# Forgetting attention with both heads' halves in one stationary block: the value product of the second head group reshaped

## The chip, the cores and the metric

The kernel runs on one core of one Trainium2 chip. The metric is the device time of one execution in microseconds. TensorE (PE) multiplies a stationary block, loaded into its array beforehand, by moving columns and writes into PSUM banks. VectorE (DVE) and ScalarE (ACT) work on PSUM and SBUF, GpSimd (POOL) on SBUF, and SyncE (SP) issues nearly all transfers.

## The reference, cut to what matters

One decoder layer on 256 tokens of width 2048: a combined input projection, two groups of 16 attention heads of 64 channels, an output projection, a gated feed-forward part with a short convolution, and norms around each. The second group, called fox in the code, is forgetting attention:

```python
def forgetting_attention(q, k, v, log_f):
    c = lax.cumsum(log_f, axis=1)
    ...
        s = jnp.einsum('bqhd,bshd->bhqs', q_blk, k).astype(jnp.float32) * scale
        s = s + c_blk[..., None] - cT[:, :, None, :]
        s = jnp.where((q_pos[:, None] >= k_pos[None, :])[None, None], s, -jnp.inf)
        p = jax.nn.softmax(s, axis=-1)
        return jnp.einsum('bhqs,bshd->bqhd', p.astype(v.dtype), v)
...
    o_b = rmsnorm(o_b.reshape(B, S, D_FOX), grp_fox_g[l])
    mix = jnp.concatenate([o_a, o_b], axis=-1) @ w_out[l]
```

## The kernel before

Every float32 operand of a matmul is split into a high part (`hi`, a rounded copy) and a low part (`lo`, what is left), and a product is summed from the passes high by high, high by low and low by high. The weights go this way too: SP loads a unit of 128x1024 into `raw` (`w_load`, L69; five buffers), ACT casts it into `whi` (L112, five buffers), DVE subtracts and writes `wlo` (L115), PE uses both.

TensorE's order is the order in which the code is written (it is scheduled by hand); the other engines' queues are ordered by the framework's scheduler, and each engine works through its own queue strictly in order. Attention is woven into the projections: `tick()` is called every few matmuls, and `later(n, f)` runs `f` after n more ticks. For a pair of heads `attend` registers four steps: `tables` (POOL builds the additive table in `p`), `scores` (L475, then softmax on DVE and ACT), `transposes` (probabilities turned by PE, L510, and split into high `ph`, L312, and low `pl`, L313), and `pv` (values times probabilities). For the fox group, two pairs at a time follow a q and a k projection of 256 columns each (`proj_T`); after the fourth two, the remaining steps run inside `out_half(0)`, the first half of the output projection. There a weight unit is 12 matmuls of 512 columns, with a tick after the sixth and the last. Steps of one pair use rotating PSUM banks of the tag `att`, four in all.

In `pv` of a fox pair, `weighted` before the change uses as stationary block the values of both heads (2 x 64 channels), high or low, and as moving columns both heads' probabilities (2 x 256 queries; in the second key block 2 x 128). Three passes over two key blocks are six matmuls (L534, L536) into one bank. Of its four quarters the two in which head and probability belong together are used. ACT then writes the gained high part into `oT` (L545) and the square into `sqo` (L546), DVE the low part of `oT` (L547), each once per head on 64 partitions, and POOL adds the square to `sqs` (L553). The first attention group already has `shared` value heads: four matmuls (L522, L524), ACT copies the lower half of the bank into `olow` (L527), DVE adds halves (L530), and then the same chain on 128 partitions.

When all fox pairs are done, `group_rstd(1)` sums `sqs` over channels with four small matmuls (L681). It is registered four ticks after the last `pv`:

```python
        later(stages(6, 1)[2] + 4, lambda: group_rstd(1, rstd_b))
```

After `out_half(0)` the attention pool is given back. `gbc_mix` (L726) is laid into its room, and `x_sb` (L729, two loads) into that of the values `vpb`; both are loaded by SP, in the same queue as the weight units.

Of the kernel before, what the change touches and what calls it, by code (L numbers as in the profile page):

```python
# [8 lines left out]
F32 = mybir.dt.float32  # L9
F32R = mybir.dt.float32r  # L10
BF16 = mybir.dt.bfloat16
AF = mybir.ActivationFunctionType
ALU = mybir.AluOpType
# [4 lines left out]
P = 128  # L18
# [13 lines left out]
def hybrid_layer(ctx: ExitStack, tc: tile.TileContext, x, pre_mix_g, w_in, b_forget, sinks,  # L32
# [3 lines left out]
    pe, act, dve, pool, sp = nc.tensor, nc.scalar, nc.vector, nc.gpsimd, nc.sync  # L36
# [12 lines left out]
    def bank(tag="acc"):  # L49
        return ps.tile([P, 512], F32, tag=tag, bufs=4, name="bank_" + tag)  # L50
# [264 lines left out]
    with tc.tile_pool(name="mixp", bufs=1) as mp:  # L315
# [110 lines left out]


        vpa = ap.tile([P, 2, 2, P], F32R, tag="vpa", name="vpa")
        vpb = main.tile([P, 2, 2, 8, P], F32R, tag="x", name="vpb")

        NK = 3
        keys = ap.tile([P, 2 * NK, S], F32R, tag="keys", name="keys")
# [26 lines left out]
        def attend(j, q, ki, values, table, h0, sink, at, shared=False):  # L459


            qh, ql = q
            kh, kl = khi[ki], klo[ki]
            st = {}

            def scores():


                p = st["p"]
                sb = [bank("att") for _ in range(2)]  # L470
                passes = ((qh, kh), (ql, kh), (qh, kl))
                for cs, t, nk in ((slice(0, 256), 1, 256), (slice(256, 384), 0, P)):
                    for n, (a, b) in enumerate(passes):
                        for e, r in enumerate(halves):
                            pe.matmul(sb[e][:, cs], a[r, t * P:(t + 1) * P], b[r, 0:nk],  # L475
                                      start=(n == 0), stop=(n == 2))

                nm = small.tile([P, 2, 2], F32, tag="nm", name="nm")
                for t, cs in tiles:
                    for e in range(2):  # L480
                        dve.tensor_tensor_reduce(
                            p[:, e, cs], sb[e][:, cs], p[:, e, cs], -1.0,
                            nsnk[:, h0 + e:h0 + e + 1] if sink else -NEG,
                            ALU.add, ALU.min, nm[:, t, e:e + 1])
                rs = small.tile([P, 2, 2], F32, tag="rs", name="rs")
                if sink:
                    es = small.tile([P, 2, 2], F32, tag="es", name="es")
                    sk = snk[:, h0:h0 + 2].unsqueeze(1).to_broadcast([P, 2, 2])
                    dve.tensor_tensor(es, nm, sk, op=ALU.add)
                    act.activation(es, es, AF.Exp)  # L490
                for t, cs in tiles:
                    for e in range(2):
                        act.activation(p[:, e, cs], p[:, e, cs], AF.Exp, bias=nm[:, t, e:e + 1],
                                       scale=-1.0, accum_out=rs[:, t, e:e + 1])
                if sink:
                    dve.tensor_tensor(rs, rs, es, op=ALU.add)
                dve.reciprocal(rs, rs)
                for t, cs in tiles:
                    for e in range(2):
                        dve.tensor_scalar(p[:, e, cs], p[:, e, cs], rs[:, t, e:e + 1], None,  # L500
                                          op0=ALU.mult)

            def transposes():
                p = st["p"]
                st["h"] = ap.tile([P, 2, 384], F32R, tag="ph", name="ph")
                st["l"] = ap.tile([P, 2, 384], F32R, tag="pl", name="pl")
                for e in range(2):
                    pb = bank("att")
                    for i, c in enumerate((256, 0, P)):
                        pe.transpose(pb[:, i * P:(i + 1) * P], p[:, e, c:c + P], ident)  # L510
                    split(st["h"][:, e, :], st["l"][:, e, :], pb[:, :384])

            def weighted():

                ph, pl = st["h"], st["l"]
                o = bank("att")
                ov = o.rearrange("p (e q) -> p e q", e=2)
                first, second = slice(0, 256), slice(256, 384)
                if shared:

                    for n, p in enumerate((ph, pl)):
                        pe.matmul(ov, values(0), p[:, :, first], start=(n == 0), stop=False)  # L522
                    for n, p in enumerate((ph, pl)):
                        pe.matmul(ov[:, :, P:256], values(1), p[:, :, second], start=False,  # L524
                                  stop=(n == 1))
                    low = ap.tile([64, 2, 256], F32, tag="olow", name="olow")
                    act.copy(low, ov[64:128])  # L527
                    s = scratch()
                    for e, r in enumerate(halves):
                        dve.tensor_tensor(s[r, :], ov[0:64, e, :], low[:, e, :], op=ALU.add)  # L530
                    return [(slice(0, P), s)]
                passes = ((0, ph), (1, ph), (0, pl))
                for n, (hl, p) in enumerate(passes):
                    pe.matmul(ov, values(hl, 0), p[:, :, first], start=(n == 0), stop=False)  # L534
                for n, (hl, p) in enumerate(passes):
                    pe.matmul(ov[:, :, P:256], values(hl, 1), p[:, :, second], start=False,  # L536
                              stop=(n == 2))
                return [(r, ov[r, e, :]) for e, r in enumerate(halves)]

            def pv():  # L540
                sq = ap.tile([P, 256], F32, tag="sqo", bufs=1, name="sqo")
                for r, o in weighted():
                    g = gcol[r, 32 + j:33 + j]
                    hi, lo = oT[j][r, 0:256], oT[j][r, 256:512]
                    act.activation(hi, o, AF.Copy, scale=g)  # L545
                    act.activation(sq[r, :], o, AF.Square)  # L546
                    dve.scalar_tensor_tensor(lo, o, g, hi.bitcast(F32), op0=ALU.mult,  # L547
                                             op1=ALU.subtract)
                acc = sqs[:, j // 8, :]
                if j % 8 == 0:  # L550
                    pool.tensor_copy(acc, sq)
                else:
                    pool.tensor_tensor(acc, acc, sq, op=ALU.add)  # L553

            def tables():
                st["p"] = ap.tile([P, 2, 384], F32, tag="p", bufs=2, name="p")
                table(st["p"])

            for n, f in zip((max(at[0] - 3, 1),) + at, (tables, scores, transposes, pv)):
                later(n, f)  # L560
# [14 lines left out]
        def fox_pair(p, q, ki, at):  # L575
            def table(t):
                cb = ap.tile([P, 2, 256], F32, tag="cb", bufs=2, name="cb")
                sp.dma_start(cb.rearrange("p e k -> p (e k)"),
                             c_dram[2 * p:2 * p + 2, :].rearrange("e k -> (e k)")
                             .partition_broadcast(P))  # L580
                for e in range(2):
                    h = 2 * p + e
                    pool.tensor_scalar(t[:, e, 0:256], cb[:, e, :], -1.0, cq[:, 1, h:h + 1],
                                       op0=ALU.mult, op1=ALU.add)
                    pool.tensor_scalar(t[:, e, 256:384], cb[:, e, 0:P], -1.0, cq[:, 0, h:h + 1],
                                       op0=ALU.mult, op1=ALU.add)

                v = t[:, :, P:384]
                pool.affine_select(out=v, in_=v, compare_op=ALU.is_ge, fill=NEG, base=0,
                                   pattern=[[0, 4], [-1, P]], channel_multiplier=1)  # L590

            attend(8 + p, q, ki, lambda hl, t: vpb[:, hl, t, p, :], table, 2 * p, False, at)

        def stages(n, m):
            return n, n + 6 + 3 * m, n + 9 + 4 * m
# [35 lines left out]
        for p0, npair, cols in ((0, 3, 384), (3, 3, 384), (6, 2, 272)):  # L631
# [11 lines left out]
                    if kt % 4 != 0:  # L643
                        tick()
            for t, b in enumerate(b2):
                bv = b[:, :npair * P].rearrange("p (j c) -> p j c", c=P)
                vh, vl = vpb[:, 0, t, p0:p0 + npair, :], vpb[:, 1, t, p0:p0 + npair, :]
                act.activation(vh, bv, AF.Copy, scale=rpre[t])
                dve.scalar_tensor_tensor(vl, bv, rpre[t], vh.bitcast(F32), op0=ALU.mult,
                                         op1=ALU.subtract)  # L650
                if cols == 272:
                    dve.scalar_tensor_tensor(z[:, t, :], b[:, 256:272], rpre[t], bfb,
                                             op0=ALU.mult, op1=ALU.add)
# [593 lines left out]
```

## Time and profile before

| | |
|---|---|
| median of 3 runs | 1063.57 us (1063.05 to 1065.51) |
| profiled execution, span from first to last instruction | 1062.6 us |
| busy: PE, PE weight loads, DVE, ACT, POOL | 1049.6, 914.6, 839.7, 639.1, 229.3 us |
| fox attention and what it is woven into | about 172 to 272 us of the span |
| mean granted TensorE clock | 0.996 |

The span is the profiled execution's own time; the median of the runs is 0.97 us more, which is what lies around it. In rows of the timeline the columns are start in us, length in us, engine, line, operation, output and inputs, shape and count; what stands in brackets is the idle time ahead and what ended it. Rows of matmuls overlap at their ends, so that the distance between two starts is the cost of one, not its length. In groups by line the last columns are busy time, mean length in ns, and idle time ahead.

### The profile page before, as it was taken

To read this page: it belongs to the slowest core of one execution; us is meant where nothing else is said; L and a number is where in the kernel's file an instruction comes from. 1 tells how busy PE (TensorE), PEld (TensorE's weight loads), DVE (VectorE), ACT (ScalarE), POOL (GpSimd) and SP (SyncE) were. 2 spreads that over 40 slices of the span, in tenths; PEclk is the share of its full clock that TensorE was granted. 3 is DMA by queue.
4 is the path that set the end of the run, shared out by engine and by line. 5 is a ranking of instruction groups with operands and counts; after the bars stand their busy time and mean duration, and the time that the engine had idled before them with its cause. 6 is when DMAs were issued, how large, how long until landed. Compare 5 with 4: busy or idle time off the path is not lost.

```text
span 1062.6 us, 16272 instructions
## 1 busy us (share of the span) xinstructions
PE 1049.6 (99%) x5890; PEld 914.6 (86%) x5890; DVE 839.7 (79%) x1369; ACT 639.1 (60%) x1096; POOL 229.3 (22%) x256
## 2 busy tenths in 40 slices
PE   9999999999999999999999999999999999999996
PEld 7889988888889888888888888888888888888885
DVE  5988887887467887787767999668778687789987
ACT  6767667776556765566655556446556565556551
POOL 4253335441022121211212000002121121200004
PEclk9999999999999999999999999999999999999998
DMA  8745566555773876656665666666566665656563
GB/s 280 217 120 168 162 209 202 165 170 162 282 236 107 280 231 187 193 180 185 211 188 188 193 204 206 213 196 190 169 209 188 197 197 180 194 179 200 194 242 121
DMA packets 154285, 207.08 MB, mean 195 GB/s; under 512 B 6845, under 2 KB 131037, under 8 KB 153181
## 3 DMA queue, kind: packets, MB, share of 16 engines
q1 hardware_dynamic: 153200, 203.37, 60.7%
q10 hardware_dynamic: 1004, 2.68, 0.6%
q8 instruction: 46, 0.75, 0.3%
q14 instruction: 35, 0.28, 0.1%
HBM read 201.68 MB, written 4.21 MB: 194 GB/s over the span
## 4 chain that ended last, share of the span: by engine, by line
PE 84%; DVE 9%; issue 2%; DMA 2%; ACT 2%; POOL 1%; DVEq 0%; SPq 0%; POOLq 0%; ACTq 0%
PE bank_acc L284 15%; PE bank_att L284 14%; PE bank_acc L309 12%; PE bank_att L967 9%; PE bank_acc L290 8%; PE bank_att L290 7%; PE bank_acc L253 7%; DVE wlo L313 4%; PE bank_acc L258 4%; PE bank_acc L967 2%; PE bank_att L475 1%; PE bank_att L510 1%; DVE wlo L115 1%; PE bank_acc L932 1%; DMA raw<-in_w_down_dram 1%
## 5 line engine op out<-in xcount | busy, mean ns | idle before, releaser
L115 DVE TENSOR_TENSOR wlo<-raw,whi 128x1024 fp32r<-128x1024 f32 (+3 forms) x271 | 328.5, 1224 | 127.0 <-ACT whi L112 118.4
L112 ACT CAST whi<-raw 128x1024 fp32r<-128x1024 f32 (+3 forms) x270 | 273.2, 1029 | 131.8 <-issue 88.8
L899 POOL TENSOR_TENSOR room<-room,rowf 128x256 f32<-128x256 f32 x88 | 100.3, 1160 | 393.9 <-DVE room L898 392.0
L284 PE MATMUL bank_acc<-hT,whi 128*128 128x512 f32 x736 | 173.3, 390 | 0.0
L284 PEld LDWEIGHTS bank_acc<-hT,whi 128*128 128x128 f32 x736 | 136.4, 188 | 27.4
L967 PE MATMUL bank_att<-whi,G 128*128 128x512 f32 x488 | 156.0, 389 | 0.0
L284 PE MATMUL bank_att<-hT,whi 128*128 128x512 f32 x640 | 150.6, 390 | 0.0
L284 PEld LDWEIGHTS bank_att<-hT,whi 128*128 128x128 f32 x640 | 118.7, 188 | 23.9
L967 PEld LDWEIGHTS bank_att<-whi,G 128*128 128x128 f32 x488 | 91.6, 188 | 18.9
L967 PE MATMUL bank_att<-wlo,G 128*128 128x512 f32 x244 | 95.0, 389 | 0.2 <-DVE wlo L313 0.2
L290 PEld LDWEIGHTS bank_acc<-hT,wlo 128*128 128x128 f32 x736 | 89.3, 188 | 2.0
L290 PE MATMUL bank_acc<-hT,wlo 128*128 128x256 f32 x736 | 89.8, 279 | 0.0
L901 ACT ACTIVATE room<-room,cw 128x256 f32<-128x256 f32 x88 | 53.0, 602 | 60.6 <-POOL room L899 60.6
L253 PE MATMUL bank_acc<-hT,whi 128*128 128x512 f32 x352 | 88.0, 395 | 0.0
L309 PE MATMUL bank_acc<-whi,oT 128*128 128x512 f32 (+1 forms) x272 | 81.7, 379 | 0.0
L290 PEld LDWEIGHTS bank_att<-hT,wlo 128*128 128x128 f32 x640 | 77.6, 188 | 1.7
L290 PE MATMUL bank_att<-hT,wlo 128*128 128x256 f32 x640 | 77.9, 279 | 0.0
L903 DVE SCALAR_TENSOR_TENSOR room<-room,cw 128x256 f32<-128x256 f32 x88 | 62.4, 709 | 17.6 <-ACT room L901 17.3
L253 PEld LDWEIGHTS bank_acc<-hT,whi 128*128 128x128 f32 x352 | 63.3, 188 | 11.5
L313 DVE TENSOR_TENSOR wlo<-raw,whi 128x1024 fp32r<-128x1024 f32 (+1 forms) x56 | 61.3, 1119 | 12.1 <-ACT whi L312 12.1
L312 ACT CAST whi<-tb 128x1024 fp32r<-128x1024 f32 x42 | 44.0, 1050 | 43.0 <-PE bank_att L967 19.6
L312 ACT CAST whi<-raw 128x1024 fp32r<-128x1024 f32 (+1 forms) x56 | 52.3, 958 | 27.1 <-PE bank_att L967 20.6
(254 smaller groups left out, 1594.0 us busy)
## 6 DMA issues: line engine op xcount, KB each, us to landing
raw<-in_w_up_dram SPq DMA_DIRECT2D x176, 512.0 KB, 4.2
raw<-in_w_down_dram SPq DMA_DIRECT2D x58, 512.0 KB, 4.7
raw<-in_w_in_dram SPq DMA_DIRECT2D x51, 512.0 KB, 4.7
raw<-in_w_out_dram SPq DMA_DIRECT2D x32, 512.0 KB, 4.6
extra<-in_w_down_dram SPq DMA_DIRECT2D x20, 512.0 KB, 4.7
raw<-in_w_in_dram SPq DMA_DIRECT2D x16, 384.0 KB, 3.6
tb<-in_w_down_dram SPq DMA_DIRECT2D x10, 512.0 KB, 3.5
cb<-c_dram SPq DMA_DIRECT2D x8, 256.0 KB, 3.8
```

Of the source, the lines that this page charges most:

```text
L112: i1 = act.copy(hi[:, cs], raw[:, cs])
L115: i2 = dve.tensor_tensor(lo[:, cs], raw[:, cs], hi[:, cs].bitcast(F32), op=ALU.subtract)
L253: pe.matmul(b, parts[u][0][:, a, m * P:(m + 1) * P], hT[:, kt, :], start=(kt == 0), stop=(kt == KT - 1))
L284: pe.matmul(b, parts[u][0][:, a, m * P:(m + 1) * P], hT[:, kt, :], start=(kt == 0), stop=(kt == KT - 1))
L290: pe.matmul(b[:, 256:512], parts[u][1][:, a, m * P:(m + 1) * P], hT[:, kt, 0:256], start=False, stop=False)
L309: pe.matmul(b, a, r[:, cols], start=(first and i == 0), stop=(last and i == 2))
L312: act.copy(hi, src)
L313: dve.tensor_tensor(lo, src, hi.bitcast(F32), op=ALU.subtract)
L899: pool.tensor_tensor(u[:, 2:258], u[:, 2:258], rowf, op=ALU.mult)
L901: act.activation(y, u[:, 2:258], AF.Identity, bias=cw[:, 3, ch:ch + 1], scale=cw[:, 2, ch:ch + 1])
L903: dve.scalar_tensor_tensor(y, u[:, 1:257], cw[:, 1, ch:ch + 1], y, op0=ALU.mult, op1=ALU.add)
L967: pe.matmul(b[:, to] if to else b, a, r[:, cols], start=(first and i == 0), stop=(last and i == 2))
```

## The change

For a fox pair the two heads are now treated one after the other. The stationary block of one head is its high and its low values side by side (2 x 64 channels), the moving columns are its high and low probabilities side by side. Two matmuls per head, into a bank of its own, give all four products in four quarters; three are summed, and the quarter low by low is not used. For each head ACT copies one quarter from partitions 64 to 127 into `olow`, DVE adds the second quarter to it and then the third, into `osum`. From `osum`, on 128 partitions, ACT makes the high part of `oT`, DVE the low part, and ACT squares `osum` in place, after DVE has read it. To make the blocks contiguous, `vpb` is laid out by head and then high and low, and `ph` and `pl` become two views of one tile `phl`.

```diff
-        vpb = main.tile([P, 2, 2, 8, P], F32R, tag="x", name="vpb")
+        vpb = main.tile([P, 2, 8, 2, 2, 64], F32R, tag="x", name="vpb")
...
-                st["h"] = ap.tile([P, 2, 384], F32R, tag="ph", name="ph")
-                st["l"] = ap.tile([P, 2, 384], F32R, tag="pl", name="pl")
+                both = ap.tile([P, 2, 2, 384], F32R, tag="phl", name="phl")
+                st["h"], st["l"] = both[:, :, 0, :], both[:, :, 1, :]
+                st["both"] = both
...
-                passes = ((0, ph), (1, ph), (0, pl))
-                for n, (hl, p) in enumerate(passes):
-                    pe.matmul(ov, values(hl, 0), p[:, :, first], start=(n == 0), stop=False)
-                for n, (hl, p) in enumerate(passes):
-                    pe.matmul(ov[:, :, P:256], values(hl, 1), p[:, :, second], start=False,
-                              stop=(n == 2))
-                return [(r, ov[r, e, :]) for e, r in enumerate(halves)]
+                s = ap.tile([P, 256], F32, tag="sqo", bufs=1, name="osum")
+                low = ap.tile([64, 2, 256], F32, tag="olow", name="olow")
+                for e, r in enumerate(halves):
+                    if e:
+                        o = bank("att")
+                        ov = o.rearrange("p (e q) -> p e q", e=2)
+                    p = st["both"][:, e]
+                    pe.matmul(ov, values(e, 0), p[:, :, first], start=True, stop=False)
+                    pe.matmul(ov[:, :, P:256], values(e, 1), p[:, :, second], start=False,
+                              stop=True)
+                    act.copy(low[:, e, :], ov[64:128, 0, :])
+                    dve.tensor_tensor(low[:, e, :], ov[0:64, 0, :], low[:, e, :], op=ALU.add)
+                    dve.tensor_tensor(s[r, :], ov[0:64, 1, :], low[:, e, :], op=ALU.add)
+                return [(slice(0, P), s)]
...
                     act.activation(hi, o, AF.Copy, scale=g)
-                    act.activation(sq[r, :], o, AF.Square)
+                    if shared:
+                        act.activation(sq[r, :], o, AF.Square)
                     dve.scalar_tensor_tensor(lo, o, g, hi.bitcast(F32), op0=ALU.mult,
                                              op1=ALU.subtract)
+                    if not shared:
+                        act.activation(sq, o, AF.Square)
```

The scheduler orders ACT, DVE, POOL and SP anew around the fox pairs. TensorE, at the last pair (the matmuls of `out_half(0)` stand around it; - is before, + is now):

```order
 L309 MATMUL bank_acc<-wlo,oT_117 128x512
 L309 MATMUL bank_acc<-whi,oT_117 128x512
-L534 MATMUL bank_att<-ph,vpb 128x512 x2
-L534 MATMUL bank_att<-pl,vpb 128x512
-L536 MATMUL bank_att<-ph,vpb 128x2x128 x2
-L536 MATMUL bank_att<-pl,vpb 128x2x128
+L540 MATMUL bank_att<-phl,vpb 128x512
+L541 MATMUL bank_att<-phl,vpb 128x2x128
+L540 MATMUL bank_att<-phl,vpb 128x512
+L541 MATMUL bank_att<-phl,vpb 128x2x128
 L309 MATMUL bank_acc<-whi,oT_118 128x512
 L309 MATMUL bank_acc<-wlo,oT_118 128x512
```

Three matmuls of 512 and three of 256 columns become two and two, at the same place among the others.

DVE at the last pair (`oT_130` is its output), before:

```order
L115 TENSOR_TENSOR wlo<-raw,whi 128x1024 x2
L547 SCALAR_TENSOR_TENSOR oT_130<-bank_att,gcol,oT_130 64x256 x2
L115 TENSOR_TENSOR wlo<-raw,whi 128x1024 x2
L181 TENSOR_SCALAR rv<-bank_att 128x1 x2
```

and now:

```order
L115 TENSOR_TENSOR wlo<-raw,whi 128x1024 x2
L544 TENSOR_TENSOR olow<-bank_att,olow 64x256 x2
L545 TENSOR_TENSOR osum<-bank_att,olow 64x256 x2
L115 TENSOR_TENSOR wlo<-raw,whi 128x1024
L559 SCALAR_TENSOR_TENSOR oT_130<-osum,gcol,oT_130 128x256
L115 TENSOR_TENSOR wlo<-raw,whi 128x1024
L181 TENSOR_SCALAR rv<-bank_att 128x1 x2
```

Four adds come in, and a subtraction of a weight unit now stands between them and the low part of `oT`.

ACT at the same place, before:

```order
L545 ACTIVATE oT_130<-bank_att,gcol 64x256
L546 ACTIVATE sqo<-bank_att 64x256
L545 ACTIVATE oT_130<-bank_att,gcol 64x256
L546 ACTIVATE sqo<-bank_att 64x256
L112 CAST whi<-raw 128x1024 x2
```

and now:

```order
L543 COPY olow<-bank_att 64x256 x2
L112 CAST whi<-raw 128x1024
L556 ACTIVATE oT_130<-osum,gcol 128x256
L562 ACTIVATE osum<-osum 128x256
L112 CAST whi<-raw 128x1024
```

A cast of a weight unit now stands between the copies out of the banks and the high part and the square.

SP, at the loads that wait for the end of attention:

```order
-L69 DMA raw<-in_w_out_dram 128x2x512 x18
-L729 DMA x_sb<-in_x_dram 128x2048
-L726 DMA gbc_mix<-in_post_mix_g_dram 128x2048
-L729 DMA x_sb<-in_x_dram 128x2048
-L69 DMA raw<-in_w_out_dram 128x2x512 x13
+L69 DMA raw<-in_w_out_dram 128x2x512 x17
+L744 DMA x_sb<-in_x_dram 128x2048 x2
+L741 DMA gbc_mix<-in_post_mix_g_dram 128x2048
+L69 DMA raw<-in_w_out_dram 128x2x512 x14
```

Both loads of `x_sb` now stand ahead of `gbc_mix`, and one weight unit more stands behind these three.

More of the change, by code (lines that the diff above doesn't have):

```diff
@@ L531, in weighted @@
                     return [(slice(0, P), s)]
-                passes = ((0, ph), (1, ph), (0, pl))
-                for n, (hl, p) in enumerate(passes):
-                    pe.matmul(ov, values(hl, 0), p[:, :, first], start=(n == 0), stop=False)
-                for n, (hl, p) in enumerate(passes):
-                    pe.matmul(ov[:, :, P:256], values(hl, 1), p[:, :, second], start=False,
-                              stop=(n == 2))
-                return [(r, ov[r, e, :]) for e, r in enumerate(halves)]
+                s = ap.tile([P, 256], F32, tag="sqo", bufs=1, name="osum")
[12 more added lines that the diff above has]
+                return [(slice(0, P), s)]
             def pv():
-                sq = ap.tile([P, 256], F32, tag="sqo", bufs=1, name="sqo")
+                if shared:
+                    sq = ap.tile([P, 256], F32, tag="sqo", bufs=1, name="sqo")
                 for r, o in weighted():
+                    if not shared:
+                        sq = o
                     g = gcol[r, 32 + j:33 + j]
@@ L545, in pv @@
                     act.activation(hi, o, AF.Copy, scale=g)
-                    act.activation(sq[r, :], o, AF.Square)
+                    if shared:
+                        act.activation(sq[r, :], o, AF.Square)
                     dve.scalar_tensor_tensor(lo, o, g, hi.bitcast(F32), op0=ALU.mult,
                                              op1=ALU.subtract)
+                    if not shared:
+                        act.activation(sq, o, AF.Square)
                 acc = sqs[:, j // 8, :]
@@ L590, in table @@
                                    pattern=[[0, 4], [-1, P]], channel_multiplier=1)
-            attend(8 + p, q, ki, lambda hl, t: vpb[:, hl, t, p, :], table, 2 * p, False, at)
+            attend(8 + p, q, ki, lambda e, t: vpb[:, t, p, e], table, 2 * p, False, at)
         def stages(n, m):
@@ L645, in hybrid_layer @@
             for t, b in enumerate(b2):
-                bv = b[:, :npair * P].rearrange("p (j c) -> p j c", c=P)
-                vh, vl = vpb[:, 0, t, p0:p0 + npair, :], vpb[:, 1, t, p0:p0 + npair, :]
+                bv = b[:, :npair * P].rearrange("p (j e c) -> p (j e) c", e=2, c=64)
+                vh, vl = (vpb[:, t, p0:p0 + npair, :, i, :].rearrange("p j e c -> p (j e) c")
+                          for i in range(2))
                 act.activation(vh, bv, AF.Copy, scale=rpre[t])
```

## The prediction

> **What bounds the kernel now.** I read the page's busy times, then busy time by stage, then who waits for whom on PE in the stage of the change, then the timeline there.
>
> ```profile
> PE 1049.6 (99%) x5890; PEld 914.6 (86%) x5890; DVE 839.7 (79%) x1369; ACT 639.1 (60%) x1096; POOL 229.3 (22%) x256
> PE 84%; DVE 9%; issue 2%; DMA 2%; ACT 2%; POOL 1%; DVEq 0%; SPq 0%; POOLq 0%; ACTq 0%
> 172.00:280.00 108.00, 108.00 (x643) 93.39 (x642) 81.71 (x173) 73.77 (x158) 40.02 (x54) 1.00 0.59 185
> 940.00:1062.60 122.60, 111.90 (x510) 92.85 (x508) 107.86 (x136) 60.33 (x78) 12.52 (x11) 0.97 0.54 186
> ```
>
> The first row is the page's, the second the chain that ended last; the last two are stages (stage, sum, then PE, PE loads, DVE, ACT, POOL busy, clock, DMA share, GB/s). PE works through all 108.00 us of the fox stage at a granted clock of 1.00, with no idle time; DVE has 108.00 - 81.71 = 26.3 us free there, ACT 34.2. So matmul time taken out of this stage shortens the run, as long as no new wait of PE takes its place. Everything later hangs on PE's progress through buffers: weight loads wait for buffers that PE and DVE give back, so a gain here shifts all the rest. PE's idle time is in the last stage (122.60 - 111.90 = 10.7 us), which only starts earlier.
>
> **Term 1: the matmuls.** One fox pair, and one pair of the first group, which already has the new count of two matmuls of 512 and two of 256 columns:
>
> ```profile
> 207.21 0.62 PE L534 MATMUL bank_att<-ph,vpb 128*128 128x512 f32 x2
> 207.67 0.39 PE L534 MATMUL bank_att<-pl,vpb 128*128 128x512 f32 x1
> 207.90 0.40 PE L536 MATMUL bank_att<-ph,vpb 128*128 128x256 f32 x2
> 208.26 0.82 PE L510 MATMUL bank_att<-ident,p 128*128 128x128 f32 x6
> 66.34 0.40 PE L522 MATMUL bank_att<-ph,vpa 128*128 128x512 f32 x1
> 66.80 0.28 PE L524 MATMUL bank_att<-ph,vpa 128*128 128x256 f32 x1
> 67.04 3.34 PE L253 MATMUL bank_acc<-hT,whi 128*128 128x512 f32 x14
> ```
>
> By starts, three of 512 cost 207.90 - 207.21 = 0.69, three of 256 cost 208.26 - 207.90 = 0.36: 1.05 us a pair. The first group's four cost 67.04 - 66.34 = 0.70. The columns in motion are equally wide and every matmul has a weight load in both, so I take 0.70 for the new form. Saved: 8 pairs x 0.35 = 2.8 us. It agrees with the rates of the pair itself, 0.69/3 + 0.36/3 = 0.35. The new pairs alternate 512 and 256 columns and change banks in the middle, which no row before shows; I allow 0.05 a pair for that as the lower bound, about half of one matmul of 256, and 0.01 upwards: 2.4 to 2.9 us.
>
> **Term 2: ACT, DVE and POOL.** The rows for old and new operations:
>
> ```profile
> L545 ACT ACTIVATE oT<-bank_att,gcol 64x256 fp32r<-64x256 f32 x16 | 7.5, 470 | 13.9 <-PE bank_att L536 12.2 <-DVE oT L547 1.6
> L546 ACT ACTIVATE sqo<-bank_att 64x256 f32<-64x256 f32 x16 | 5.9, 366 | 0.0
> L547 DVE SCALAR_TENSOR_TENSOR oT<-bank_att,gcol,oT 64x256 fp32r<-64x256 f32 x16 | 7.7, 482 | 6.1 <-ACT sqo L546 5.5
> L530 DVE TENSOR_TENSOR scr<-bank_att,olow x16: 406/416/418, 62.5 to 148.2; 64x256 f32<-64x256 f32 x16
> L545 ACT ACTIVATE oT<-scr,gcol x8: 502/508/512, 63.5 to 148.6; 128x256 fp32r<-128x256 f32 x8
> L547 DVE SCALAR_TENSOR_TENSOR oT<-scr,gcol,oT x8: 474/481/976, 64.3 to 149.3; 128x256 fp32r<-128x256 f32 x8
> L546 ACT ACTIVATE sqo<-scr x8: 401/401/404, 63.9 to 149.1; 128x256 f32<-128x256 f32 x8
> L553 POOL TENSOR_TENSOR sqs<-sqs,sqo x14: 737/743/1059, 70.7 to 271.8; 128x256 f32<-128x256 f32 x14
> ```
>
> ACT per pair: before 2 x 470 + 2 x 366 = 1672 ns; now two copies of 64x256 (no row of its own; nearest is the square of that shape out of PSUM, 366; bounds 366 and 470) + 508 + 401 = 1641. Nothing. DVE: before 2 x 482 = 964; now four adds of 416 + 481 = 2145, so 1.18 us a pair more, 9.4 us in eight. The cover is the 26.3 us that DVE has free; rival 3 prices its loss. POOL does the same add, later. The twelve writes of `vpb` in runs of 64 and the strides of `phl` have no row before; bounds -0.1 and +0.1 us each on engines with idle time: nothing.
>
> **Term 3: a wait ahead of the channel sums.** What gets longer is the way from the last pair's matmuls to `sqs`, and PE needs `sqs` four ticks later, in order. Before:
>
> ```profile
> 268.42 0.62 PE L534 MATMUL bank_att<-ph,vpb 128*128 128x512 f32 x2
> 269.47 0.39 PE L309 MATMUL bank_acc<-whi,oT 128*128 128x512 f32 x1
> 271.32 0.37 ACT L546 ACTIVATE sqo<-bank_att 64x256 f32<-64x256 f32 x1
> 271.72 1.05 ACT L112 CAST whi<-raw 128x1024 fp32r<-128x1024 f32 x1
> 271.84 0.74 POOL L553 TENSOR_TENSOR sqs<-sqs,sqo 128x256 f32<-128x256 f32 x1 [6.24 <-ACT sqo L546]
> 272.60 0.34 SPq L726 DMA_DIRECT2D gbc_mix<-in_post_mix_g_dram  x1
> 272.80 1.23 DVE L115 TENSOR_TENSOR wlo<-raw,whi 128x1024 fp32r<-128x1024 f32 x1 [0.58 <-ACT whi L112]
> 273.77 0.39 PE L309 MATMUL bank_acc<-wlo,oT 128*128 128x512 f32 x1
> 273.75 1.05 ACT L112 CAST whi<-raw 128x1024 fp32r<-128x1024 f32 x1 [0.98 <-PE bank_acc L309]
> 274.69 0.64 PEld L681 LDWEIGHTS bank_att<-ones,sqs 128*128 128x128 f32 x4
> 282.46 1.05 ACT L112 CAST whi<-raw 128x1024 fp32r<-128x1024 f32 x1 [1.67 <-PE bank_acc L309]
> 276.00:278.00 2.00, 2.00 (x10) 1.61 (x10) 0.29 (x3) 1.74 (x3) 1.07 (x2) 1.00 1.01 426
> ```
>
> Call the start of the pair's matmuls S (268.42). `sqs` was ready at 272.58 = S + 4.16, PE loaded it at S + 6.27: 2.1 us to spare. Now PE arrives 0.35 earlier, at S + 5.92. The new chain: the first head's bank is done at S + 0.23 + 0.28, two copies of 0.37 end at about S + 1.3, the four adds by S + 2.7 (three starts about 0.34 apart behind the first, as two adds in a row overlap), but in the queues shown above ACT then casts a weight unit, and DVE subtracts that unit, ahead of the pair's own work. That cast needs the buffer of the unit in which the pair lies. PE finishes that unit six matmuls of 0.227 us (1.36; from 269.47 to 273.77 there are 19) behind the pair, so at S + 0.70 + 1.36 = S + 2.06; the row at 273.75 shows a cast 0.2 us after the last matmul of a unit (269.47 + 18 x 0.227 = 273.55). So: cast S + 2.26 to 3.31; subtraction 3.34 to 4.57; low part of `oT` (0.48) to 5.05; the square may only then overwrite `osum` (0.40, with a hand-over of 0.05) to 5.5; POOL 0.15 later (271.69 to 271.84), 0.74, to 6.39; PE's load a little behind that. Against S + 5.92 a wait of 0.5 us. Bounds: 0, if the cast finds its buffer free and the unit's subtraction ends 0.6 earlier; 1.7, if the add falls behind one more subtraction (1.23). I take 0.5, which the rows give directly.
>
> **SP.** `gbc_mix` waits for POOL's last add, in a queue ahead of the weight units. It moves from S + 4.18 to about S + 6.5, and one unit more is behind it. That unit's cast came at 282.46 before, S + 14; the three megabytes ahead of it, at the burst's 426 GB/s, are 7.4 us from about S + 1, and with `gbc_mix` asked for only at S + 6.5 the unit lands at an estimated S + 11 to 13. Five buffers lie between its cast and its use by PE, some four units of 2.7 us. Nothing, with that cover; gone, a late unit would cost PE at most the 2.3 us of the shift.
>
> **Sum.** -2.8 + 0.5 = -2.3 us against the span, 1062.6 to 1060.3. The median of the runs shown is 0.97 above that span: 1063.57 - 2.3 = 1061.3 us. A measurement of this kernel tells about 0.2% (2.1 us) from no change, so the border of "faster" is 1061.4, just above the forecast.
>
> **The rivals.**
> 1. *No wait at the sums.* The cast's buffer is free sooner, or the chain is half a microsecond shorter: the whole 2.8 is kept, 1060.8. For it: 0.5 is small against six hand-overs in a row. Against it: the buffer's release is PE's, and PE's pace is even.
> 2. *A longer wait at the sums.* POOL's operation stretches while DVE works on SBUF operands:
>
> ```profile
> 202.96 2.35 DVE L115 TENSOR_TENSOR wlo<-raw,whi 128x1024 fp32r<-128x1024 f32 x2
> 203.11 2.46 POOL L583 TENSOR_SCALAR p<-cb,cq 128x256 f32<-128x256 f32 x1 [1.49 <-PE bank_att L510]
> 205.91 0.48 POOL L583 TENSOR_SCALAR p<-cb,cq 128x256 f32<-128x256 f32 x1
> ```
>
> The same instruction takes 2.46 us behind two subtractions and 0.48 without. If the next unit's subtraction starts ahead of the last add, the add ends up to 1.2 us later: wait 1.7, 1062.5. Against it: that subtraction needs the cast behind the square, 1.05 us, while the add needs 0.15 + 0.74 = 0.89 from the same point; it escapes by 0.16 us.
> The Trainium skill ("SBUF — State Buffer", section "Who interferes with whom") says that a DVE instruction with two SBUF inputs shuts out a GpSimd instruction that reads SBUF, and that whichever issues first keeps the shared port for its whole length. The pair above agrees. By that rule the low part of `oT`, now read from `osum` in SBUF rather than from a bank, joins those that shut POOL out; the sum by the rule stays at -2.3 where the add escapes and is -1.1 where it does not.
> 3. *DVE becomes the bound: slower.* The place is the split of the first pair's probabilities in fox groups two to four:
>
> ```profile
> 205.23 1.01 DVE L313 TENSOR_TENSOR pl<-bank_att,ph 128x384 fp32r<-128x384 f32 x2
> ```
>
> It ends at 206.24, and PE needs it at 207.21: 0.97 us to spare. If nothing of the 2 x 1.18 a group is absorbed, and DVE also stands idle for one cast of 1.05 that ACT has ahead of the copies, DVE is 3.41 late, PE waits 2.44 in each of three groups, 7.3 us: 1063.57 - 2.3 + 7.3 = 1068.6. It decides against the change from 2.3/3 + 0.97 = 1.7 us of lateness a group. Against it: queued through the rows between two groups, DVE would by the durations above reach the next scores an estimated 0.3 us late.
> 4. *The saving doesn't appear*: PE meets small waits elsewhere (new semaphores on the second head's matmuls) that eat it, 0.35 us a pair: 1063.6. Against it: PE had no idle time in front of the same kind of waits in 108 us.
>
> **Chances.** Forecast (wait 0.2 to 0.8; 1061.0 to 1061.6) 0.42; rival 1 0.20; rival 2 0.22; rival 3 0.08; rival 4 0.08. Faster by over 0.2%: 0.20 + two thirds of the forecast, 0.29 = 0.49. Same: 0.13 + 0.22 + 0.08 = 0.43. Slower: 0.08. The range goes from rival 1 with the upper bound of term 1 and some scatter, 1060.3, to short of rival 4, 1063.4; outside lie rivals 3 and 4 and little else.
>
> **What would show it.** The fox pairs' matmuls at 0.70 by starts; DVE's busy time about 9 us higher in the fox stage, with PE at 100% until the sums; ahead of the four matmuls of the channel sums an idle PE of about 0.5 us, released by POOL; the last add 2.2 us later after the pair's matmuls than before. Wrong: idle PE ahead of a fox pair's matmuls (rival 3), or a weight unit of the output projection waiting for its transfer.

## The result, and the profile after

| | before | changed |
|---|---|---|
| median of 21 runs each | 1064.11 us (1063.05 to 1066.43) | 1062.77 us (1062.12 to 1064.49) |
| ratio, 95% interval | | 0.9985 (0.9979 to 0.9991): -1.6 us (-2.2 to -1.0) |
| span of the profiled execution | 1062.6 us | 1062.0 us |
| mean granted TensorE clock | 0.996 | 0.996 |

Microseconds beside a ratio, here and below, are worked out from the ratio, which is estimated from the runs and is not the quotient of the two medians (these differ by 1.3 us here). The changed kernel is a little faster, by less than the 2.3 us that were forecast, which lie just outside the interval. 1062.77 lies in the predicted range; a change of -0.15% falls into what the prediction called the same. Of the 1.5 us between forecast and result, 0.5 is the base: with 21 runs the kernel before stands at 1064.11, not 1063.57.

The page's busy times and the chain that ended last, and the fox stage (stage, sum, then PE, PE loads, DVE, ACT, POOL busy, clock, DMA share, GB/s):

```profile
PE 1047.4 (99%) x5874; PEld 911.7 (86%) x5874; DVE 849.2 (80%) x1393; ACT 638.4 (60%) x1096; POOL 227.5 (21%) x256
PE 75%; DVE 15%; issue 3%; ACT 3%; DMA 2%; POOL 1%; DVEq 0%; SPq 0%; POOLq 0%; ACTq 0%
172.00:277.00 105.00, 104.58 (x620) 89.69 (x619) 87.92 (x197) 72.73 (x156) 41.04 (x53) 1.00 0.58 185
```

DVE is busy 9.5 us longer over the whole run. PE, which had no gap in this stage, now has 0.42 us of idle time in it. The chain's larger share of DVE is not read here: in a second profile of the same kernel it was 11%, and it comes from the down projections, far behind this stage. PE's matmul records:

```profile
259.70 0.50 PE L540 MATMUL bank_att<-phl,vpb 128*128 128x512 f32 x1 [0.37 <-DVE phl L313]
...
266.76 0.40 PE L540 MATMUL bank_att<-phl,vpb 128*128 128x512 f32 x1
...
267.45 0.39 PE L309 MATMUL bank_acc<-whi,oT 128*128 128x512 f32 x1
```

The last pair costs 267.45 - 266.76 = 0.69 us, as forecast. The seventh pair (the first of fox group four) waits for DVE's split of the probabilities, which the forecast had not put in. PE's weight loads, grouped by what they waited for (total, times, longest), name it again, with the channel sums (L696):

```profile
PEld bank_att L540 <- DVE phl L313: 1.0, 2, 0.8
...
PEld bank_att L696 <- POOL sqs L567: 0.5, 1, 0.5
```

A load's wait overlaps the matmul before it, so these are not yet lost time (the loads of the scores, L475, stand idle three times for 0.4 us in the kernel before, too, where PE loses nothing). To find the lost time I paired the start of every TensorE matmul outside the fox pairs in the two profiles and took how far it moved. From just ahead of the first fox pair to just behind the sums:

| place | changed against before, us |
|---|---|
| each of seven fox pairs (all but the seventh) | -0.33 to -0.37 |
| seventh pair: 0.35 saved, 0.80 waited | +0.45 |
| scores of fox group four | +0.22 |
| channel sums | +0.31 |
| all | -1.46 |

So 2.80 us were saved by the matmuls, 1.34 us given back in three waits. A second profile of the changed kernel gave -1.47 with the same three waits. This sum, called the ledger from here on, is what the experiments are read by: outside the fox stage two profiles of one kernel differ by up to 0.8 us (at the first input loads, and in the down projection), so spans of single profiles cannot settle a microsecond.

### The profile page after: what moved, and what is told of

Read it like the earlier page. It is cut to its first block, busy times and chain, and to the rows that moved or that the text cites. A ratio compares the mean times of both kernels' runs of the same rounds, so it can differ in the third digit from the quotient of the medians.

```text
span 1062.0 us, 16259 instructions
## 1 busy us (share of the span) xinstructions
PE 1047.4 (99%) x5874; PEld 911.7 (86%) x5874; DVE 849.2 (80%) x1393; ACT 638.4 (60%) x1096; POOL 227.5 (21%) x256
## 4 chain that ended last, share of the span: by engine, by line
PE 75%; DVE 15%; issue 3%; ACT 3%; DMA 2%; POOL 1%; DVEq 0%; SPq 0%; POOLq 0%; ACTq 0%
PE bank_acc L284 15%; PE bank_att L284 14%; PE bank_acc L309 10%; PE bank_acc L290 8%; PE bank_att L290 7%; PE bank_acc L253 7%; DVE wlo L313 6%; PE bank_att L982 4%; PE bank_acc L258 3%; DVE wlo L115 1%; DMA extra<-in_w_down_dram 1%; PE bank_att L475 1%; DVE tb L1026 1%; PE bank_att L511 1%; DVE tb L1023 1%
```

## The experiments

Three questions: is the saving itself whole (1); do the added operations of DVE and ACT cause the waits, or their order (2, 3, 5, 6); what does the wait at the sums cost (4). The code shown is each kernel's difference from the changed kernel; all were timed in five rounds with the kernel before on the same chip, and times and ledgers are against the kernel before.

**1. The new matmuls with the old evacuation.** Per head one quarter is read straight from its bank, as before the change; the other two quarters are not added, which leaves out two of the three partial products.

```diff
-                s = ap.tile([P, 256], F32, tag="sqo", bufs=1, name="osum")
-                low = ap.tile([64, 2, 256], F32, tag="olow", name="olow")
+                outs = []
...
-                    act.copy(low[:, e, :], ov[64:128, 0, :])
-                    dve.tensor_tensor(low[:, e, :], ov[0:64, 0, :], low[:, e, :], op=ALU.add)
-                    dve.tensor_tensor(s[r, :], ov[0:64, 1, :], low[:, e, :], op=ALU.add)
-                return [(slice(0, P), s)]
+                    outs.append((r, ov[r, 0, :]))
+                return outs
```

> The new four matmuls a fox pair in two banks, but the short way out of the banks as before: per head ACT makes the high part and the square and DVE the low part from one quarter of the bank; the other two products are left out of the sum. Theory A (the matmuls give 8 x 0.35 = 2.8 us, and the longer way out of the banks gives 1.3 of it back as waits of TensorE inside the fox stage): 2.8 us faster than before, no wait at the last group's scores, at the seventh pair or at the channel sums. Rival B (the rest is lost outside the fox stage, in the loads at the start or in the down projection): 1.6 us faster as the changed kernel, with the full 2.8 gained at the channel sums.

Measured: 1061.57 against 1064.37 us, 0.9976 (0.9967 to 0.9985), -2.6 us; ledger -2.81, no wait of PE at any pair, at the scores or at the sums.

```profile
172.00:277.00 105.00, 105.00 (x625) 90.74 (x624) 80.28 (x172) 73.90 (x157) 39.46 (x53) 1.00 0.61 189
```

The stage, columns as above: PE without a gap, DVE 7.6 us less busy than in the changed kernel. The saving is whole; all that is lost comes with the evacuation.

**2. The new evacuation with as many matmuls as before.** The first head's two matmuls are issued twice, so that a pair has six again (the first head's product is then doubled). In this kernel the scheduler also put POOL's adds to `sqs` elsewhere, behind both multiplications of the keys' row factor (L442), and moved two casts of ACT (in fox groups one and two) and one load of SP (behind the last pair).

```diff
+                    if e == 0:
+                        pe.matmul(ov, values(e, 0), p[:, :, first], start=False, stop=False)
+                        pe.matmul(ov[:, :, P:256], values(e, 1), p[:, :, second], start=False,
+                                  stop=False)
```

> The new way out of the banks, with the matmul time of before: the first head's two matmuls of each fox pair run twice, so six matmuls a pair (the first head's product is summed twice). Theory A: slower than before by what the longer way out costs when TensorE arrives 0.35 us later at each step, 0.5 to 1.3 us, as waits at the seventh pair (0.5 to 0.8), the last group's scores (up to 0.2) and the channel sums (0 to 0.3). Rival B: no difference from before within 0.3 us.

Measured: 1065.35 us, 1.0010 (1.0001 to 1.0019), +1.1 us; ledger +0.53, of which 0.32 is the wait at the sums; the other 0.2 is spread over the stage in steps below 0.03. The wait at the seventh pair, expected here, did not come. That pointed to POOL's order, the only queue entry between the fifth pair and the seventh, apart from the matmuls themselves, that differs from the changed kernel. The other half microsecond of the timed difference does not show in the fox stage; the interval, +0.1 to +2.0, holds the ledger's value too.

**3. The square into a buffer of its own.** In the changed kernel ACT squares `osum` in place, so the square must wait for DVE's low part of `oT`. Here it goes to another tile, right behind the high part. The work of all engines stays the same; the scheduler puts POOL's first add of a group back ahead of both multiplications, as in the kernel before.

```diff
-                        sq = o
+                        sq = ap.tile([P, 256], F32, tag="ql", bufs=6, name="sqb")
...
-                    if shared:
-                        act.activation(sq[r, :], o, AF.Square)
+                    act.activation(sq[r, :], o, AF.Square)
...
-                    if not shared:
-                        act.activation(sq, o, AF.Square)
```

> The changed kernel with the square written to a tile of its own (in the ring of the q low parts), so that it need not wait until DVE has read the sum; ACT squares right behind the high part. DVE's work is the same. Theory A, as I now read it (ACT stands behind DVE for the square in place, its next cast of a weight unit comes late, and DVE with it): most of the 1.3 comes back, 2.4 to 2.8 us faster than before, the waits at the seventh pair and the sums below 0.2 each. Rival C (DVE's 1.18 us more work a pair makes it late, whatever the square does): only the wait at the sums goes, 1.8 to 2.0 faster than before, and the seventh pair still waits 0.7 or more.

Measured: 1061.98 us, 0.9976 (0.9967 to 0.9985), -2.6 us; ledger -2.80, no waits. The same kernel was run again with the last experiments:

> The kernel with the square in a tile of its own once more, beside the changed kernel on the same chip: 2.4 to 2.8 us faster than before by the first measurement and by the count of the waits, about 1 faster than the changed kernel. If the first measurement was chance: 1.6 as the changed kernel.

Measured: 1061.78 against 1064.34 us, 0.9979 (0.9970 to 0.9988), -2.2 us; ledger -2.79, no waits. So DVE's 9.4 us of added work cost nothing by themselves. But two things were undone together here, the in-place square and POOL's order. Experiments 5 and 6 take them apart. (The scheduler also moved one instruction of group four's softmax on DVE and an operation of ACT on `mix_sb`, both behind the start of that softmax.)

**4. The channel sums two ticks later.**

```diff
-        later(stages(6, 1)[2] + 4, lambda: group_rstd(1, rstd_b))
+        later(stages(6, 1)[2] + 6, lambda: group_rstd(1, rstd_b))
```

> The changed kernel with the channel sums of the second group six ticks behind the last pair in place of four. Theory A and rival C: the 0.3 us at the sums comes back and nothing else, 1.8 to 1.9 us faster than before; the seventh pair waits 0.8 as in the changed kernel.

Measured: 1062.91 us, 0.9986 (0.9977 to 0.9995), -1.5 us; ledger -1.76: nothing lost at the sums any more, 0.31 better than the changed kernel, the two other waits as they were. PE's loads of the sums:

```profile
275.47 0.64 PEld L696 LDWEIGHTS bank_att<-ones,sqs 128*128 128x128 f32 x4
```

The sums start without idle time ahead. The timed difference to the changed kernel is too small to be seen; the ledger shows it.

**5. Square in place, POOL's add behind.** The adds of the first three fox groups are deferred by two ticks, and the multiplications of the keys are pinned in their order (not shown), so that the add of a group's first pair stands behind both of them. The queues of PE, ACT, DVE and SP are those of the changed kernel.

```diff
-                if j % 8 == 0:
-                    pool.tensor_copy(acc, sq)
+                def gather():
+                    if j % 8 == 0:
+                        i = pool.tensor_copy(acc, sq)
+                    else:
+                        i = pool.tensor_tensor(acc, acc, sq, op=ALU.add)
+                    if not shared:
+                        tc.keep_in_program_order(i)
+                if shared or j >= 14:
+                    gather()
...
-                    pool.tensor_tensor(acc, acc, sq, op=ALU.add)
+                    later(2, gather)
```

> The changed kernel, square in place as it is, but POOL's adds to sqs held behind both multiplications of the next k pair, in place of one between the two; the queues of ACT, DVE, SP and TensorE are the same instruction for instruction. Theory A (ACT held by the square in place, its cast late, DVE late): the seventh pair still waits, 0.5 to 0.8 us; 1.4 to 1.8 us faster than before. Rival D (the add between the two multiplications holds the second key, and DVE with it): no wait at the seventh pair nor at the last group's scores, only the 0.3 at the sums; 2.3 to 2.6 us faster than before.

Measured: 1061.74 us, 0.9978 (0.9970 to 0.9987), -2.3 us; ledger -2.49. Only the 0.31 at the sums is left; pair and scores wait no more. Timeline of POOL, ACT, DVE and PE, with the start of the sixth pair (the last of group three) and of the seventh:

```profile
237.92 2.42 POOL L442 TENSOR_TENSOR scr<-scr 128x256 f32<-128x256 f32 x2 [0.69 <-DVE scr L441]
239.87 0.40 PE L542 MATMUL bank_att<-phl,vpb 128*128 128x512 f32 x1
240.30 0.92 POOL L571 TENSOR_TENSOR sqs<-sqs,osum 128x256 f32<-128x256 f32 x1
240.36 0.41 ACT L312 CAST keys<-scr 128x256 fp32r<-128x256 f32 x1 [1.27 <-POOL scr L442]
248.70 0.42 DVE L483 CUSTOM_DVE_ANT_0 p<-bank_att,p 128x256 f32<-128x256 f32 x1
258.46 1.02 DVE L313 TENSOR_TENSOR phl<-bank_att,phl 128x384 fp32r<-128x384 f32 x2
259.33 0.40 PE L542 MATMUL bank_att<-phl,vpb 128*128 128x512 f32 x1
```

**6. Square apart, POOL's add between.** The reverse: experiment 3 with POOL's add pinned between the multiplications of the two keys, where the changed kernel has it. The other queues are those of experiment 3.

```diff
+                def gather():
...
+                if shared or j % 2 or j >= 14:
+                    gather()
...
+                    pend.append(gather)
...
+                while pend:
+                    pend.pop()()
```

> The kernel with the square in a tile of its own, but with POOL's add between the two multiplications of the next k pair, as in the changed kernel; the queues of ACT, DVE, SP and TensorE are those of the kernel with the square apart. Theory A: no wait at the seventh pair, 2.3 to 2.8 us faster than before. Rival D: the seventh pair and the last group's scores wait 0.4 to 1.0 us together; 1.6 to 2.2 faster than before.

Measured: 1062.79 us, 0.9985 (0.9976 to 0.9994), -1.6 us; ledger -2.33: a wait of 0.30 at the fifth pair and of 0.17 at the scores, none at the seventh pair and none at the sums. The order alone costs, though at another pair than in the changed kernel. The timed gain is 0.7 smaller than the ledger's; its interval holds both.

```profile
237.27 0.74 POOL L442 TENSOR_TENSOR scr<-scr 128x256 f32<-128x256 f32 x1 [0.69 <-DVE scr L441]
237.97 1.72 POOL L569 TENSOR_TENSOR sqs<-sqs,sqb 128x256 f32<-128x256 f32 x1
239.04 0.40 PE L543 MATMUL bank_att<-phl,vpb 128*128 128x512 f32 x1
239.65 0.91 POOL L442 TENSOR_TENSOR scr<-scr 128x256 f32<-128x256 f32 x1
247.85 0.41 DVE L484 CUSTOM_DVE_ANT_0 p<-bank_att,p 128x256 f32<-128x256 f32 x1
257.59 1.01 DVE L313 TENSOR_TENSOR phl<-bank_att,phl 128x384 fp32r<-128x384 f32 x2
258.68 0.40 PE L543 MATMUL bank_att<-phl,vpb 128*128 128x512 f32 x1
```

**7. The changed kernel again**, beside 5, 6 and the second run of 3:

> The changed kernel once more, beside the three others: 1.6 us faster than before, waits of 0.8 at the seventh pair, 0.2 at the last scores and 0.3 at the sums, as in its first profile, if these belong to the kernel; if they are chance of one execution, they differ.

Measured: 1062.74 us, 0.9988 (0.9979 to 0.9996), -1.3 us; ledger -1.47.

## Why the prediction was right, and where it was not

**Term 1, the matmuls: right.** 2.8 us forecast, 2.81, 2.80 and 2.79 in the three ledgers without waits. The alternation of 512 and 256 columns and the change of banks cost nothing.

**Term 3, the wait at the sums: right in every link, the wait a little too long.** The rows from the last pair's matmuls (S = 266.76) on, of ACT, DVE, POOL, SP and PE's loads:

```profile
269.01 1.05 ACT L112 CAST whi<-raw 128x1024 fp32r<-128x1024 f32 x1 [0.99 <-PE bank_acc L309]
270.10 1.22 DVE L115 TENSOR_TENSOR wlo<-raw,whi 128x1024 fp32r<-128x1024 f32 x1 [0.75 <-ACT whi L112]
271.24 0.48 DVE L559 SCALAR_TENSOR_TENSOR oT<-osum,gcol,oT 128x256 fp32r<-128x256 f32 x1
271.81 0.42 ACT L562 ACTIVATE osum<-osum 128x256 f32<-128x256 f32 x1 [1.34 <-DVE oT L559]
272.31 0.74 POOL L567 TENSOR_TENSOR sqs<-sqs,osum 128x256 f32<-128x256 f32 x1 [5.67 <-ACT osum L562]
273.07 0.33 SPq L741 DMA_DIRECT2D gbc_mix<-in_post_mix_g_dram  x1
273.09 0.52 PEld L696 LDWEIGHTS bank_att<-ones,sqs 128*128 128x128 f32 x4 [0.47 <-POOL sqs L567]
```

Cast at S + 2.25 (forecast 2.26), subtraction at 3.34 (3.34), low part done at 4.96 (5.05), square done at 5.47 (5.5), add done at 6.29 (6.39), load at 6.33. Against PE's forecast arrival at S + 5.92 that is 0.41. The four loads then take 0.52 instead of 0.64, which leaves 0.29, near the 0.31 of the ledger. Forecast 0.5: mis-sized by 0.2. Experiments 3, 5 and 6 show the cause: with the square apart the wait is gone, whatever POOL's order, and with POOL's order alone undone (experiment 5) it stays at 0.31. SP's `gbc_mix` went out at S + 6.31 (6.5), and no unit of the output projection came late: nothing, as forecast.

**Term 2, ACT, DVE and POOL "nothing": the step that failed.** Its durations for ACT and DVE hold (groups of the stage: busy, mean ns, idle time ahead):

```profile
L567 POOL TENSOR_TENSOR sqs<-sqs,osum 128x256 f32<-128x256 f32 x7 | 7.9, 1124 | 40.5 <-ACT osum L562 40.5
L545 DVE TENSOR_TENSOR osum<-bank_att,olow 64x256 f32<-64x256 f32 x16 | 6.6, 411 | 0.3
L544 DVE TENSOR_TENSOR olow<-bank_att,olow 64x256 f32<-64x256 f32 x16 | 5.9, 406 | 0.0
L543 ACT COPY olow<-bank_att 64x256 f32<-64x256 f32 x16 | 5.5, 370 | 7.8 <-PE bank_att L541 7.7
L559 DVE SCALAR_TENSOR_TENSOR oT<-osum,gcol,oT 128x256 fp32r<-128x256 f32 x8 | 4.0, 504 | 0.0
```

The copy is 370 ns (taken as 366), the adds 406 and 411 (416), and DVE's total rose by 9.5 us (9.4). Experiment 3 does all that work without a wait, so the cover of 26.3 us held too. What failed is "POOL does the same add, later". Neither the orders shown with the change nor the working of the prediction gives the order of POOL's queue around the pairs. The seven adds of the stage took 801 ns in the mean before and now take 1124: three of them are stretched to between 1.5 and 1.7 us, the others are not longer. And the add does not only come later, it stands elsewhere in POOL's queue. POOL between the fifth and the sixth pair, before:

```profile
238.74 0.74 POOL L553 TENSOR_TENSOR sqs<-sqs,sqo 128x256 f32<-128x256 f32 x1
239.44 2.42 POOL L442 TENSOR_TENSOR scr<-scr 128x256 f32<-128x256 f32 x2
```

and in the changed kernel, followed to the seventh pair with rows of DVE, ACT and PE:

```profile
237.75 0.74 POOL L442 TENSOR_TENSOR scr<-scr 128x256 f32<-128x256 f32 x1 [0.94 <-DVE scr L441]
238.44 1.72 POOL L567 TENSOR_TENSOR sqs<-sqs,osum 128x256 f32<-128x256 f32 x1
239.44 0.40 PE L540 MATMUL bank_att<-phl,vpb 128*128 128x512 f32 x1
240.12 0.92 POOL L442 TENSOR_TENSOR scr<-scr 128x256 f32<-128x256 f32 x1
241.07 0.41 ACT L312 CAST keys<-scr 128x256 fp32r<-128x256 f32 x1 [2.15 <-POOL scr L442]
244.27 0.85 DVE L545 TENSOR_TENSOR osum<-bank_att,olow 64x256 f32<-64x256 f32 x2
244.94 0.69 PE L475 MATMUL bank_att<-keys,qh 64*128 64x128 f32 x4
246.30 0.48 DVE L559 SCALAR_TENSOR_TENSOR oT<-osum,gcol,oT 128x256 fp32r<-128x256 f32 x1
246.81 0.42 ACT L562 ACTIVATE osum<-osum 128x256 f32<-128x256 f32 x1 [1.14 <-DVE oT L559]
247.14 1.03 ACT L112 CAST whi<-raw 128x1024 fp32r<-128x1024 f32 x1
248.20 1.22 DVE L115 TENSOR_TENSOR wlo<-raw,whi 128x1024 fp32r<-128x1024 f32 x1 [1.42 <-ACT whi L112]
249.34 0.42 DVE L481 CUSTOM_DVE_ANT_0 p<-bank_att,p 128x256 f32<-128x256 f32 x1
259.10 1.01 DVE L313 TENSOR_TENSOR phl<-bank_att,phl 128x384 fp32r<-128x384 f32 x2
```

Read downwards: the add for `sqs`, stretched to 1.72 us, holds up the second key's multiplication. ACT stands idle 2.15 us before it can cast that key (1.27 in experiment 5), and everything behind it in ACT's and DVE's queues moves back, DVE's adds out of the sixth pair's banks with it. The last of them ends at 245.12, and the scores that need its bank wait 0.2: the four matmuls from 244.94 on take 0.69 us, in experiment 3, where the adds end ahead of the scores, 0.45. Then comes the second delay: the square may not start until DVE has read `osum`, the next unit's cast stands behind the square, DVE stands idle 1.42 us for that cast, and the softmax of group four is behind it. Its split ends at 260.11, too late for PE. Ahead of group three's softmax the square stands behind the next unit's cast (at 219.40, the cast at 218.16), so the second delay is missing there, and no pair of that group waits.

How the two add up can be read from the start of the softmax (L481 here) and from the end of the split, counted from the start of the sixth pair. The rows of experiment 3:

```profile
239.67 0.40 PE L540 MATMUL bank_att<-phl,vpb 128*128 128x512 f32 x1
245.38 0.86 POOL L564 TENSOR_TENSOR sqs<-sqs,sqb 128x256 f32<-128x256 f32 x1 [5.08 <-ACT sqb L557]
245.56 0.96 DVE L558 SCALAR_TENSOR_TENSOR oT<-osum,gcol,oT 128x256 fp32r<-128x256 f32 x1
247.58 0.41 DVE L481 CUSTOM_DVE_ANT_0 p<-bank_att,p 128x256 f32<-128x256 f32 x1
257.33 1.01 DVE L313 TENSOR_TENSOR phl<-bank_att,phl 128x384 fp32r<-128x384 f32 x2
259.13 0.40 PE L540 MATMUL bank_att<-phl,vpb 128*128 128x512 f32 x1
```

| kernel | square | POOL's add | softmax | split ends | PE's seventh pair | ledger |
|---|---|---|---|---|---|---|
| experiment 3 | apart | first | +7.91 | +18.67 | +19.46 | -2.80 |
| experiment 5 | in place | behind | +8.83 | +19.61 | +19.46 | -2.49 |
| experiment 6 | apart | between | +8.81 | +19.56 | +19.64 | -2.33 |
| changed | in place | between | +9.90 | +20.67 | +20.26 | -1.46 |

In group four each delay alone makes the softmax 0.9 us late, both together 2.0; from there to the end of the split it is 10.8 us in all four kernels. That the single buffer of `osum` comes free later with the square in place plays no part: DVE's 16 adds into it (L545) stand idle for 0.3 us in all. PE needs the first head's half of the split, which ends some 0.5 us before the whole: at +18.2 in experiment 3, 1.3 us ahead of PE. One delay fits into these 1.3 us, two do not, and the pair waits 0.8. My first theory, the in-place square alone, fell with experiment 5; the order of POOL's queue alone does not make the seventh pair wait either, by experiment 6. Experiment 6 waits at the fifth pair by the same kind of sum, one group earlier. Counted from the fourth pair, its softmax of group three starts at +6.92 (+5.93 in experiment 3, +6.12 in the changed kernel), and the two heads' halves of the split end at +19.69 and +20.15; PE would be there at +19.67 and, for the second head, 0.35 later. Of the 0.80 against the changed kernel, 0.48 is DVE's low part of `oT`, which with the square apart runs beside POOL's add and takes 0.96 us instead of 0.48.

**The rivals.** Rival 1 (no wait at the sums) did not hold. Rival 2 (a longer wait there) did not either: the last add kept its 0.74 us. Its mechanism was real, but at other adds, the longest 1.72 us beside DVE's subtraction, in the middle of the stage. This agrees with the rule of the Trainium skill that the prediction cited ("SBUF — State Buffer", section "Who interferes with whom"). Rival 3 had the right place and the right kind (the first pair's split late, and a wait only once the spare time is used up; it is 1.3 us in group four, counted to the first head's half, with which PE now starts; the prediction had 0.97 to the whole split). It happened in one group of three, for 0.8 us instead of 2.44, and not because DVE had too much work. Its 0.08 was too little for the mild form, in which some, not all, of the lateness is absorbed. Rival 4's 0.35 a pair did not occur.

**Right in the number, in part by luck.** The prediction's own sign of being wrong, idle PE ahead of a fox pair's matmuls, did appear. The waits at the seventh pair and the scores, 1.0 us together, are in no term of its sum. The range reached far enough for them because it also takes in a longer wait at the sums (rival 2, 1062.5), which did not come.

**The best version** is experiment 3: -2.6 and -2.2 us against before in two measurements, with nothing given back in the fox stage. In the batch that held both, its median lies 0.96 us below the changed kernel's (1061.78 and 1062.74); their intervals against before overlap, and it is the ledger, 1.3 us better both times, that tells them apart. Experiment 5 is as fast by its median (1061.74); only its ledger, with the 0.31 at the sums, puts it behind.

## What to carry to other kernels

When work on the bound engine is cut, go through the queues of the engines that feed it in their new order, instruction by instruction, and not only through their busy totals: an engine idle for half its time can still be late. An update in place makes the writer wait for a reader on another engine (ACT 1.14 us for DVE here), and all that is queued behind the writer waits too; a separate buffer took that away here. Delays on feeding engines cost nothing until they add up to the spare time ahead of the bound engine, so count them together, from one common start.

## What the hardware showed that was not expected

POOL and DVE slow each other in both directions. In the changed kernel POOL's add took 1.72 us beside DVE's subtraction (0.74 with DVE idle), and DVE's next instruction on two SBUF inputs then took longer as well, 0.96 against 0.42 for the same one two microseconds later:

```profile
237.91 1.65 DVE L115 TENSOR_TENSOR wlo<-raw,whi 128x1024 fp32r<-128x1024 f32 x1
239.49 0.96 DVE L313 TENSOR_TENSOR keys<-scr,keys 128x256 fp32r<-128x256 f32 x1
241.51 0.42 DVE L313 TENSOR_TENSOR keys<-scr,keys 128x256 fp32r<-128x256 f32 x1 [1.07 <-ACT keys L312]
```

In the kernel before, the first of these two splits of a key took 0.95 us as well, beside POOL's second multiplication; the add is not the only instruction of POOL that does this. Experiment 3 shows the same at its own add: DVE's low part of `oT` takes 0.96 us beside POOL's 0.86, against 0.48 in the changed kernel. So a POOL add that is moved to a new place can move a cost onto DVE as well.
